# A two-layer f32 decoder trunk: the output projections in another order of products, loads and row sums

## The chip, the cores and the metric

The kernel runs on 1 core of one Trainium2 chip, in one launch. The metric is the device time in microseconds, lower is better. TensorE (PE) multiplies matrices into PSUM, VectorE (DVE) and ScalarE (ACT) work on tiles in SBUF and PSUM, GpSimd (POOL) issues transfers here and copies a little, and SyncE (SP) only issues transfers. Every engine takes its own instructions strictly in order and waits for the others through semaphores.

## The reference

The input is `x` of 512 tokens by 2048 channels in f32. Two layers follow, each of which adds a mixer's output to `x`:

```
x <- x + W_out( mixer(rms_norm(x)) * silu(gate) )
layer 0: gated differential attention, 8 heads of 256 value channels;
         o = rms_norm(o, subln_w) * (1 - lambda_init), per head
layer 1: RWKV-7 time mixing, 32 heads of 64 channels, group norm on y
```

What matters here is the end of each layer: `y` (512 x 2048) times `W_out` (2048 x 2048), plus the residual.

## The kernel before

**f32 products.** A product of f32 matrices is three matmuls of a faster format. Each operand is split into a high part (an ACT cast, `wh` for weights at L109, `hH` for rows at L475) and a low part (a DVE subtraction, `wl` at L110, `hL` at L476). `mm3` (L116) issues high x high, high x low, low x high; all of PE's matmul rows of a product bear its line, L118. Weights come from HBM in blocks of 256 by 512 (512 KB, tile `wraw`, three buffers in turn; `load_w`, issued at L76).

**The rows.** `y` comes turned, channel by token, in 16 row blocks of 128 channels by 512 tokens. All but the last come from HBM (`yd`, `yd2`), where the earlier heads left them, and `Feed` splits them ahead of use. The last two row blocks stay on the core. In layer 0 they are those of head 7, whose attention (`attention`, L386) is stepped through between the matmuls of the output projection by a `Chain`: for each of four token tiles scores, softmax, the product `o`, then `weigh` (L429: ACT squares `o`, DVE takes the root in 11 small operations through `rsqrt`, L58, and scales to `G` at L441), then `turn_y` (L443: PE transposes `G` into `yt` at L446, ACT copies it to the rows' tile `Tt` at L450). After all four tiles `split_row` (L471) splits the two row blocks whole, `hH` at L475. In layer 1 the last rows come from the last pair of heads: the last steps of the solver and the scan (which read the tiles `TT` and write `Y`), the group norm (`yc` scaled at L1757), transposes of `yc` at L1769, the gate, `split_row`.

**The output stage.** `outputs_of` (L916) makes the 2048 output columns in two halves, `one` (columns 0 to 1023) and `two`, each a `Blocks` (L804). A half is a two by two grid of places, tokens by columns: 11, 12, 21, 22 (256 tokens by 512 columns each). Of the 16 row blocks 12 go through a scheme with 7 products in place of 8 (three steps of two row blocks for each product, 36 matmuls) and 4 go plainly (`plain`, row blocks 6, 7 and 14, 15; 14 and 15 are the last rows). The 7 products are "11" and "12" (named for the block of rows that they use), "S1", "S2", "S4", "S3" (with sums of rows) and "22". `Forms` (L760) loads the rows for the sums (`load`, L770, on POOL's queue) and makes S1 to S4 (`make`, L773: DVE adds at L780, ACT and DVE splits at L793 and L794). The matching sums of weights grow in place in three tiles `Ts`: a transfer that adds to what lies there (`add_w`, L799, issued at L801), which only POOL's queue does here.

The order of the code is the order of the work on PE:

```
two.first12 / one.first12 alternately, one.first11, last rows (finish), S1 made,
one.rest: plain 6 c1, plain 14 c1, S1, plain 6 c2, plain 14 c2, S2, S4, S3, 22
two.first11, two.rest: the same again
```

(c1 and c2 are the half's two column blocks.) Between S4 and S3 stands nothing, and S3's first weights are the tile that S4 has just used, with one more block added by `add_w`.

**Residual.** The first product to reach a place writes it by `copy` (L836): an ACT copy from PSUM to SBUF, then a transfer on POOL's queue that adds `x` (layer 1: the stored `xd`) to it (L842). The others add by `take` (L845) on DVE, at L848.

Of the kernel before, what the change touches and what calls it, by code (L numbers as in the profile page):

```python
# [23 lines left out]
P = 128  # L24
# [33 lines left out]
def rsqrt(g, out, v, n, tag):  # L58
# [7 lines left out]
    for i in range(3):  # L66
        nc.vector.tensor_mul(t[:], y, y)
        nc.vector.scalar_tensor_tensor(t[:], t[:], -0.5, v, ALU.mult, ALU.mult)
        o = out if i == 2 else y
        nc.vector.scalar_tensor_tensor(o, t[:], 1.5, y, ALU.add, ALU.mult)  # L70

# [314 lines left out]
def attention(g, h, qkT, qkL, sq, vg, gap, rows=None, yT=None):  # L386
# [42 lines left out]
    def weigh(t):  # L429
# [9 lines left out]
        rsqrt(g, ro[:], so[:], 1, "r1")  # L439
# [13 lines left out]

    for i in range(NT + 3):
# [12 lines left out]
    if yT is not None:  # L467
        rows += [split_row(g, yT[:, c, :]) for c in range(2)]
# [14 lines left out]
class Feed:  # L483
# [17 lines left out]
    def __call__(self, n, m):  # L501
        self.split(n + 1, m)
        self.load(n + self.ring)

# [255 lines left out]
class Forms:  # L760


    def __init__(self, g, src, raws, homes):
        self.g, self.src, self.raws, self.homes = g, src, raws, homes
        self.at = {nm: [None] * len(homes) for nm in ("S1", "S2", "S3", "S4")}

    def load(self, i):
        for r, kb in zip(self.raws[i], (0, 1)):
# [4 lines left out]
    def make(self, nm):  # L773

        nc = self.g.nc
        for i, homes in enumerate(self.homes):
# [3 lines left out]
            nc.vector.tensor_tensor(out=o, in0=x, in1=y, op=op)  # L780
# [23 lines left out]
class Blocks:  # L804
# [26 lines left out]
    def plain(self, k0, c, *outs):  # L831
        wt = split_w(self.g, None, KG, 512, 0, self.load(k0, c))
        for out, t0, first, end in outs:
            self.products(out, self.block(k0, t0), wt, first, end)

    def copy(self, nm, ps, sign=1.0):  # L836
        nc, (t, c) = self.g.nc, PLACES[nm]
        with self.g.tc.high_priority(offset=SCAN):
            for i in range(2):
                nc.scalar.activation(self.acc(nm)[i], ps[i][:], AF.Copy, scale=sign)  # L840
                r0 = (2 * t + i) * P
                nc.gpsimd.dma_start(out=self.acc(nm)[i], accum_op=ALU.add,  # L842
                                    in_=self.x[r0 : r0 + P, self.c1 + c * 512 : self.c2 + c * 512])
# [6 lines left out]
    def first11(self, i):  # L850
        if not i:
            self.X = self.banks(0)
        load_w(self.g, self.Ts[i], self.w[self.c1 // 512], FIRST[0] + i * KG, slice(0, KG))
        self.prod(self.X, i, "11", self.Ts[i], i == 0, i == NS // KG - 1)
        add_w(self.g, self.Ts[i], self.w, FIRST[0] + i * KG, self.c2)
        if i == NS // KG - 1:
            self.take("11", self.X)

    def first12(self, i, bank):
        if not i:  # L860
            self.y = self.banks(bank)
        if i < NS // KG:
            self.prod(self.y, i, "12", self.load(FIRST[1] + i * KG, self.c1), i == 0)
        else:
            self.plain(PLAIN[0], self.c1, (self.y, 0, False, True))
            self.copy("11", self.y)

    def rest(self, begin=None, then=lambda nm: None):
# [5 lines left out]
        y, z = self.banks(1), self.banks(2)  # L874
# [4 lines left out]
        self.copy("21", z)  # L879
        then("S2")  # L880
        y, z = self.banks(1), self.banks(2)
# [3 lines left out]
        self.copy("22", y)  # L885
# [7 lines left out]
        self.copy("12", X, -1.0)  # L893
# [7 lines left out]
        self.done("12")  # L901
        for i in range(N):
# [4 lines left out]
        z = self.banks(2)  # L907
# [8 lines left out]
def outputs_of(g, one, two, feed, finish, begin=None):  # L916
# [6 lines left out]
    for i in range(N + 1):  # L923
        for x, (b, bank) in enumerate(((two, 0), (one, 1))):
            pace(s)
            b.first12(i, bank)
            s += KG
        if i == 1:
            one.sums.load(0)
    for i in range(N):  # L930
        pace(s)
        pace(s + 1)
        one.first11(i)
        s += KG
        if i:
            one.sums.load(i)
    finish(g.m)
    one.sums.make("S1")
    one.rest(then=one.sums.make)
    for i in range(N):  # L940
        two.first11(i)
# [3 lines left out]
def loader(g, w, homes):  # L945

    homes = list(homes)

    def load(k0, c):
        homes.append(homes.pop(0))  # L950
        pool, tag, bufs = homes[-1]
        raw = pool.tile([P, KG, 512], F32, name="wraw", tag=tag, bufs=bufs)
# [13 lines left out]
def layer0(g, aps):  # L966
# [3 lines left out]
    with ExitStack() as cx:  # L970
# [77 lines left out]
        with tc.issue_after(g.made[9][1]):  # L1048
            nc.vector.tensor_scalar(g.subw[:], g.subw[:], 1.0 - LAMBDA_INIT, None, ALU.mult)
# [4 lines left out]
    with ExitStack() as cx:  # L1054
# [22 lines left out]
        feed, rows = g.feed, g.feed.rows  # L1077
        ch = Chain(g, attention(g, NH - 1, *before, 20, rows, Tt[:, 4:6]), 8)
# [14 lines left out]
        def store_x(cb, t):  # L1093
            xr = xs[cb][:, t, :]
            junk = g.ps.tile([P, 512], F32, name="junkx", tag="pb")
# [12 lines left out]
        sums = Forms(g, g.yd, ((sx[0], sx[1]), (sx[2], Tt[:, 6:8]), (Tt[:, 0:2], Tt[:, 2:4])), homes)  # L1108
# [10 lines left out]
        def banks(i):  # L1119
            if i < 2:  # L1120
                return [g.pp.tile([P, 512], F32, name="pp", tag="pp") for _ in range(2)]
            return [g.ps.tile([P, 512], F32, name="z", tag="pa", bufs=2) for _ in range(2)]

        load = loader(g, aps["da_w_out"], ((g.wraw, "wraw", 3),))
# [42 lines left out]
        def begin(m):  # L1167
# [4 lines left out]
            for cb in range(1, 4):  # L1172
                for t in range(2):
# [4 lines left out]
                        [flat(g.C), flat(g.S), T2], banks, done_of(c)) for c in (0, 2)]  # L1178
# [795 lines left out]
```

## Time and profile before

| what | value |
|---|---|
| median of 3 runs | 2125.43 us (2124.93 to 2126.13) |
| profiled execution | 2125.24 us |
| its span, first to last instruction | 2123.1 us |
| mean granted clock of TensorE | 0.985 of full |
| busy: PE, DVE, ACT, POOL | 97%, 80%, 62%, 22% |
| layer 0's output stage | about 728 to 931 us |
| layer 1's output stage | about 1905 to 2118 us |

A row of a timeline gives start, duration, engine, line, operation, the tile written and those read, their shapes, and in brackets the time in which the engine was idle before it and whose instruction ended that. Matmuls overlap, so the pace is read from their starts. The granted clock is the share of full speed that PE was given in a stretch. A row of the windows view gives a stretch, its length, the busy time and count of PE, PE's weight loads, DVE, ACT and POOL, the clock, the mean busy share of the 16 DMA engines, and GB/s.

### The profile page before, as it was taken

Reading aid. Unit: us, or ns where it says so; the run is one execution under the profiler, and the core shown is the slowest. Engines: PE = TensorE matmul, PEld = TensorE weight load, DVE = VectorE, ACT = ScalarE, POOL = GpSimd, SP = SyncE. Lnnn points to the kernel's source line nnn. Section 1 sums busy time; section 2 is a strip of 40 time slices with the busy share of each in tenths; the row PEclk is TensorE's granted clock in tenths of the full one; section 3 lists DMA queues with packets and bytes.
Section 4 is the critical chain, followed back from the end, with each engine's and each line's share of the span. In section 5 each row is a group of like instructions: output and inputs, shape, how many; then the busy total and the mean of one; then the engine's idle time right before and its main releaser. Section 6 shows DMA issues by size and latency. Waiting matters only on the chain. (4 is left out here: it accounts for less than half of the span.)

```text
span 2123.1 us, 35355 instructions
## 1 busy us (share of the span) xinstructions
PE 2054.2 (97%) x11852; PEld 1686.2 (79%) x11852; DVE 1698.9 (80%) x4423; ACT 1317.8 (62%) x3119; POOL 471.3 (22%) x789
## 2 busy tenths in 40 slices
PE   9999999999999969999999999999999999997898
PEld 8878888888887857878778888888888888876676
DVE  5979788797888984576888888888888888887554
ACT  5667676676767754555666666666666666656343
POOL 0020220201203012201232322223222332333211
PEclk9999999999999989999999999999999999999899
DMA  6487887977879667952222222222222222246796
GB/s 197 118 168 181 160 176 176 172 180 158 185 175 221 197 147 155 215 134 91 77 73 78 78 78 75 80 81 78 83 77 83 74 83 77 91 143 164 161 215 141
DMA packets 104005, 281.23 MB, mean 132 GB/s; under 512 B 12848, under 2 KB 29376, under 8 KB 103824
## 3 DMA queue, kind: packets, MB, share of 16 engines
q0 software_dynamic: 32208, 99.21, 25.9%
q1 hardware_dynamic: 57184, 163.77, 24.4%
q10 hardware_dynamic: 14432, 16.01, 2.2%
q8 instruction: 93, 1.52, 0.3%
q14 instruction: 88, 0.72, 0.1%
HBM read 262.94 MB, written 15.99 MB: 131 GB/s over the span
## 5 line engine op out<-in xcount | busy, mean ns | idle before, releaser
L118 PE MATMUL pp<-hH,wh 128*128 128x512 f32 x1024 | 416.7, 407 | 0.0
L118 PE MATMUL pp<-hL,wh 128*128 128x512 f32 x1024 | 411.9, 402 | 0.0
L118 PE MATMUL pp<-hH,wl 128*128 128x512 f32 x1024 | 411.6, 402 | 0.0
L109 ACT CAST wh<-wraw 128x512 fp32r<-128x512 f32 (+1 forms) x408 | 250.3, 618 | 205.5 <-PE pp L118 110.3
L110 DVE TENSOR_TENSOR wl<-wraw,wh 128x512 fp32r<-128x512 f32 (+1 forms) x408 | 289.0, 711 | 101.7 <-ACT wh L109 96.2
L118 PE MATMUL pp<-wh,hH 128*128 128x512 f32 x696 | 278.0, 400 | 12.2 <-ACT wh L109 8.5
L118 PE MATMUL pp<-wl,hH 128*128 128x512 f32 x696 | 275.4, 396 | 0.8 <-DVE wl L616 0.6
L118 PE MATMUL pp<-wh,hL 128*128 128x512 f32 x696 | 273.8, 394 | 0.0
L118 PEld LDWEIGHTS pp<-hH,wh 128*128 128x128 f32 x1024 | 192.8, 188 | 38.0 <-issue 2.1
L118 PEld LDWEIGHTS pp<-hH,wl 128*128 128x128 f32 x1024 | 193.1, 189 | 33.3
L118 PEld LDWEIGHTS pp<-hL,wh 128*128 128x128 f32 x1024 | 193.1, 189 | 31.3
L118 PE MATMUL pp<-wh,S 128*128 128x512 f32 x672 | 214.7, 395 | 0.0
L615 ACT CAST wh<-T 128x512 fp32r<-128x512 f32 x224 | 137.3, 621 | 93.6 <-PE pp L118 71.7
L1686 POOL COPY SA<-VS 64x64 f32<-64x64 f32 x224 | 77.0, 344 | 510.8 <-DVE VS L1704 456.1
L616 DVE TENSOR_TENSOR wl<-T,wh 128x512 fp32r<-128x512 f32 x224 | 150.9, 687 | 24.9 <-ACT wh L615 24.2
L118 PEld LDWEIGHTS pp<-wh,hH 128*128 128x128 f32 x696 | 131.5, 189 | 40.5 <-ACT wh L109 8.9
L588 POOL DMA_DIRECT2D T<-in_da_w_in_dram x84 | 72.2, 859 | 387.5 <-DMA wraw<-in_da_w_in_dram 193.8
L118 PEld LDWEIGHTS pp<-wl,hH 128*128 128x128 f32 x696 | 131.7, 189 | 26.8 <-DVE wl L110 1.1
L118 PEld LDWEIGHTS pp<-wh,hL 128*128 128x128 f32 x696 | 131.8, 190 | 26.6
L1551 DVE SCALAR_TENSOR_TENSOR tmpl<-LT,n,Tm 128x60 f32<-128x60 f32 (+24 forms) x496 | 135.8, 274 | 13.4
L118 PEld LDWEIGHTS pp<-wh,S 128*128 128x128 f32 x672 | 124.7, 188 | 24.7 <-ACT wh L615 0.4
L118 PE MATMUL pp<-wl,S 128*128 128x512 f32 x336 | 132.1, 393 | 0.2 <-DVE wl L616 0.2
(380 smaller groups left out, 4335.2 us busy)
## 6 DMA issues: line engine op xcount, KB each, us to landing
wraw<-in_rw_w_in_dram SPq DMA_DIRECT2D x128, 512.0 KB, 3.7
T<-in_da_w_in_dram POOLq DMA_DIRECT2D x84, 512.0 KB, 6.5
wraw<-in_da_w_in_dram SPq DMA_DIRECT2D x64, 512.0 KB, 4.1
T<-in_da_w_in_dram SPq DMA_DIRECT2D x28, 512.0 KB, 4.4
wraw<-in_da_w_out_dram SPq DMA_DIRECT2D x22, 512.0 KB, 5.6
wraw<-in_rw_w_out_dram SPq DMA_DIRECT2D x22, 512.0 KB, 4.5
wraw<-in_da_w_in_dram POOLq DMA_DIRECT2D x21, 512.0 KB, 6.7
TT<-in_rw_w_out_dram POOLq DMA_DIRECT2D x12, 512.0 KB, 5.8
```

The costliest lines, as they stand in the source:

```text
L109: nc.scalar.copy(hi[:], raw[:, k : k + n])
L110: g.split = nc.vector.tensor_sub(lo[:], raw[:, k : k + n], hi[:].bitcast(F32)).ins
L118: m = nc.tensor.matmul(out, a, b, start=s, stop=e, skip_group_check=skip)
L588: self.g.nc.gpsimd.dma_start(out=raw, in_=src, accum_op=ALU.add)
L615: g.nc.scalar.copy(hi[:], raw[:, k])
L616: g.nc.vector.tensor_sub(lo[:], raw[:, k], hi[:].bitcast(F32))
L1551: st = nc.vector.scalar_tensor_tensor(tt, LT[:, i : i + 1, i + 1 :].to_broadcast([P, s, n]), n2[:, i : i + 1], Tm[:, 0:s, i : i + 1].to_br ...
L1686: nc.gpsimd.tensor_copy(p.SA[r_, c - 1, :], VS[r_, c, h, :])
```

## The change

1. The order. Both halves' "12" and "11" products now come before the last rows; the 36 matmuls of `two.first11` are new in that place. S1 is made after them.
2. The last rows of layer 0 are split in two halves of 256 tokens (`split_tail`), and the second half's steps are taken between the two parts of `plain` 14 (`between`). In layer 1 the last rows' steps begin after the second of `two.first11`'s three steps.
3. The rows for the sums are loaded on SP's queue, after `one.first11`.
4. The residual is loaded plainly into the place (`want`, on SP's queue), and all products add to it by `take`. `copy` is gone.
5. `plain` 14 c2 moves from before S2 to between S4 and S3; its weights have a buffer of their own.
6. `two`'s first weight blocks are loaded twice: once into `wraw` for its "11", later into freed tiles to grow its sums from (`begin_sums`).
7. In layer 1 the tiles `Ts` go in the order TT[0], a third tile, TT[1]; before, TT[0], TT[1], the third. PSUM banks are assigned by name.
8. In layer 0's `weigh` the root has 8 operations (`rsqrt_column`), and its constant factor is in `subw`.

The number of matmuls stays. The core of the diff:

```diff
+def rsqrt_column(g, out, v):
...
+    for i, c in enumerate((3.0, 12.0, 768.0)):
+        nc.vector.scalar_tensor_tensor(t[:], y, y, v[:], ALU.mult, ALU.mult)
+        o = out[:] if i == 2 else y
+        nc.vector.scalar_tensor_tensor(o, t[:], -c, y, ALU.add, ALU.mult)
...
+    def split_tail(t0):
...
+            nc.scalar.copy(hh[:, s], yT[:, c, s])
+            g.rowsplit = nc.vector.tensor_sub(hl[:, s], yT[:, c, s], hh[:, s].bitcast(F32)).ins
+
     for i in range(NT + 3):
         if i > 2:
             turn_y(i - 3)
+        if i == 4:
+            split_tail(0)
...
-    if yT is not None:
-        rows += [split_row(g, yT[:, c, :]) for c in range(2)]
+    split_tail(2)
...
-            self.g.nc.gpsimd.dma_start(
+            self.g.nc.sync.dma_start(
                 out=r, in_=self.src[k0 * P : (k0 + KG) * P, :].rearrange("(k p) t -> p k t", p=P))
...
-    def copy(self, nm, ps, sign=1.0):
...
+    def want(self, *names):
+        for nm in names:
+            t, c = PLACES[nm]
+            for i, a in enumerate(self.acc(nm)):
                 r0 = (2 * t + i) * P
...
+                self.g.nc.sync.dma_start(out=a, in_=self.x[r0 : r0 + P, self.c1 + c * 512 : self.c2 + c * 512])
...
+    def begin_sums(self):
+        for i, T in enumerate(self.Ts):
+            load_w(self.g, T, self.w[self.c1 // 512], FIRST[0] + i * KG, slice(0, KG))
+            add_w(self.g, T, self.w, FIRST[0] + i * KG, self.c2)
...
         self.plain(PLAIN[0], c1, (z, 256, True, False))
-        self.plain(PLAIN[1], c1, (y, 0, True, True), (z, 256, False, True))
+        finish(False)
+        self.want("21", "22")
+        y = self.banks("y")
+        self.plain(PLAIN[1], c1, (y, 0, True, True), (z, 256, False, True), between=lambda: finish(True))
...
-        for n, k0 in enumerate(PLAIN):
-            self.plain(k0, c2, (z, 256, n == 0, n == 1), (y, 0, False, False))
-        self.take("22", z)
+        z = self.banks("z")
+        self.plain(PLAIN[0], c2, (z, 256, True, False), (y, 0, False, False))
+        self.want("12")
...
-            self.prod(y, i, "S4", b22[i], end=i == last)
+            self.prod(y, i, "S4", b22[i])
             add_w(g, b22[i], w, FIRST[0] + i * KG, c2)
+        self.plain(PLAIN[1], c2, (z, 256, False, True), (y, 0, False, True))
...
+        if next:
+            next.Ts = [self.sums.raws[i][j] for i, j in ((0, 0), (0, 1), (1, 0))]
+            next.begin_sums()
...
     for i in range(N):
-        two.first11(i)
+        one.sums.load(i)
+    for i in range(N):
+        two.first11(i, False)
+        if i == 1:
+            finish(None)
+    two.take("11", two.X)
+    one.sums.make("S1", g.m.ins)
+    one.rest(None, one.sums.make, finish, two)
     two.rest(begin)
...
-        Ts = [flat(x) for x in g.TT] + [g.low.tile([P, KG, 512], F32, name="T2", tag="SX", bufs=3)[:]]
+        Ts = [flat(g.TT[0]), g.low.tile([P, KG, 512], F32, name="T2", tag="SX", bufs=3)[:], flat(g.TT[1])]
```

Three places show how the instructions move. The first is PE in layer 0 at the last token tile of head 7, before the change: `o` is the tile's last product, `yt` the transposes of its result `G`, and `pp` and `hH` the plain product with the last rows.

```order
L118 MATMUL o_8797<-V_8226,at_8757 128x256
L118 MATMUL o_8797<-VL_8227,at_8757 128x256
L118 MATMUL o_8797<-V_8226,al_8758 128x256
L446 MATMUL yt_8829<-ident_82,G_8228 128x128 x2
L118 MATMUL pp_8855<-wh_8883,hH_8834 128x512
L118 MATMUL pp_8855<-wl_8884,hH_8834 128x512
```

The same place after the change, where `z_8833` is a plain product with earlier rows and `z_8862` the product that follows the transposes:

```order
L133 MATMUL o_8699<-V_8142,al_8663 128x256
L133 MATMUL pp_8742<-wh_8802,hH_8603 128x512
L133 MATMUL pp_8742<-wl_8803,hH_8603 128x512
L133 MATMUL pp_8742<-wh_8802,hL_8604 128x512
L133 MATMUL z_8833<-wh_8837,hH_7762 128x512
L133 MATMUL z_8833<-wl_8838,hH_7762 128x512
L133 MATMUL z_8833<-wh_8837,hL_7763 128x512
L133 MATMUL z_8834<-wh_8837,hH_7762 128x512
L133 MATMUL z_8834<-wl_8838,hH_7762 128x512
L133 MATMUL z_8834<-wh_8837,hL_7763 128x512
L133 MATMUL z_8833<-wh_8841,hH_7766 128x512
L133 MATMUL z_8833<-wl_8842,hH_7766 128x512
```

Before, the transposes stood directly behind the last `o`; now 15 matmuls stand between (three more `z` follow the rows shown, then `yt_8777`).

The second place is DVE around the same root, after the change. `rs_t`, `rs_i` and `ro` are the root's small operations, `G` its result, `wl` weight splits, `Tt` at L819 and `fS1` at L833 the sum S1, `xq` at L887 an add to the output.

```order
L85 SCALAR_TENSOR_TENSOR ro_8644<-rs_t_8646,rs_i_8645 128x1
L819 TENSOR_TENSOR Tt_8163<-frow_8175,Tt_8163 128x2x256
L455 SCALAR_TENSOR_TENSOR ro_8644<-ro_8644,r_8476,hrstd0_596 128x1
L125 TENSOR_TENSOR wl_8842<-wraw_8835,wh_8841 128x512
L456 SCALAR_TENSOR_TENSOR G_8144<-o_8631,ro_8644,G_8144 128x256
L833 TENSOR_TENSOR fS1_8826<-Tt_8163,fS1_8826 128x512
L887 TENSOR_TENSOR xq_8167<-xq_8167,pp_8741 128x512
L125 TENSOR_TENSOR wl_8866<-wraw_8863,wh_8865 128x512
L819 TENSOR_TENSOR Tt_8163<-Tt_8163 128x2x256
L452 TENSOR_SCALAR so_8712<-so_8712 128x1
L887 TENSOR_TENSOR xq_8168<-xq_8168,pp_8742 128x512
L79 TENSOR_SCALAR rs_i_8716<-so_8712 128x1
```

Sums, weight splits and an output add stand among the root's steps of the last two token tiles; S1 now starts between the two roots.

The third place is SP's queue in layer 0 after the change. `wraw` are weight blocks, `Tt<-yd` rows for the sums, `xq` the residual.

```order
L91 DMA wraw_8743<-in_da_w_out_dram 128x1024
L808 DMA Tt_8163<-yd_78 128x2x512
L91 DMA wraw_8765<-in_da_w_out_dram 128x1024
L91 DMA wraw_8796<-in_da_w_out_dram 128x1024
L808 DMA Tt_8163<-yd_78 128x2x512
L882 DMA xq_8165<-in_x_dram 128x512 x4
L882 DMA xq_8166<-in_x_dram 128x512 x4
L91 DMA wraw_8835<-in_da_w_out_dram 128x1024
L808 DMA Tt_8163<-yd_78 128x2x512
L91 DMA wraw_8863<-in_da_w_out_dram 128x1024
```

Rows for the sums and eight residual loads stand among the weight blocks on SP; before, both of these went through POOL's queue, the residual as transfers that add.

More of the change, by code (lines that the diff above doesn't have):

```diff
@@ L923, in outputs_of @@
     for i in range(N + 1):
-        for x, (b, bank) in enumerate(((two, 0), (one, 1))):
+        for b in (one, two):
             pace(s)
-            b.first12(i, bank)
+            if i == N - 1 and b is two:
+                b.want("11")
+            b.first12(i)
             s += KG
-        if i == 1:
-            one.sums.load(0)
+    two.take("11", two.y)
     for i in range(N):
@@ L1076, in layer0, with finish @@
         g.spare = lambda k: Tt[:, (0, 1, 2, 3, 6, 7)[k % 6]]
[L1077 to L1078 removed]
+        feed = g.feed
+        tail = []
+        ch = Chain(g, attention(g, NH - 1, *before, 18, tail, Tt[:, 4:6]), 8)
+        def finish(whole):
+            while whole is False and not tail:
+                ch.step(g)
+            if whole:
+                ch.finish(g)
+        rows = RowList(feed.rows, tail)
         g.ssx = g.const.tile([P, NT, 4], F32, name="ssx")
@@ L1117, in done_of, with banks, of @@
             return done
[L1119 to L1124, printed above, removed]
+        def banks(places):
+            def of(nm):
+                where = places[nm]
+                if where == "pp":
+                    return [g.pp.tile([P, 512], F32, name="pp", tag="pp") for _ in range(2)]
+                return [g.ps.tile([P, 512], F32, name="z", tag=t, bufs=where.count(t)) for t in where]
+            return of
+        load = loader(g, aps["da_w_out"], lambda: Tt[:, 4:6])
         rs = g.work.tile([P, NT], F32, name="rs1", tag="al", bufs=1)
```

150 lines of the change are left out of this document (87 added, 63 removed).

## The prediction

> **What bounds the kernel now.** I read the page first, then the timeline of TensorE (PE) over both output stages, then the windows around its gaps, then the timelines of VectorE (DVE), ScalarE (ACT) and GpSimd (POOL), and the DMA view, for what ended each gap. The page: engine, busy time, share; and the granted clock in 40 slices.
>
> ```profile
> PE 2054.2 (97%) x11852; PEld 1686.2 (79%) x11852; DVE 1698.9 (80%) x4423; ACT 1317.8 (62%) x3119; POOL 471.3 (22%) x789
> PEclk9999999999999989999999999999999999999899
> ```
>
> PE is the bound, idle for 2123.1 - 2054.2 = 69 us in all. The two digits of the clock that fall to 8 stand where the two output stages begin, so the question is how much of the idle time lies there. The timeline of PE (start, duration, operation; in brackets the idle time before it and who ended it), layer 0 first, from the row at 1957 on layer 1:
>
> ```profile
> 773.53 0.39 PE L118 MATMUL z<-wh,hL 128*128 128x512 f32 x1
> 787.70 0.66 PE L446 MATMUL yt<-ident,G 128*128 128x128 f32 x2 [13.78 <-DVE G L441]
> 790.50 0.41 PE L118 MATMUL o<-V,al 128*128 128x256 f32 x1
> 794.81 0.66 PE L446 MATMUL yt<-ident,G 128*128 128x128 f32 x2 [3.89 <-DVE G L441]
> 796.69 0.79 PE L118 MATMUL pp<-wh,hH 128*128 128x512 f32 x1 [1.22 <-ACT hH L475]
> ...
> 845.13 0.80 PE L118 MATMUL pp<-wh,fS 128*128 128x512 f32 x1 [2.69 <-ACT wh L109]
> ...
> 918.57 0.49 PE L118 MATMUL pp<-wh,fS 128*128 128x512 f32 x1 [2.89 <-ACT wh L109]
> ...
> 1957.63 0.80 PE L118 MATMUL pp<-wh,hH 128*128 128x512 f32 x1 [8.46 <-ACT wh L109]
> ...
> 1978.52 1.12 PE L1769 MATMUL pt<-ident,yc 128*128 128x128 f32 x4 [6.13 <-DVE yc L1757]
> 1982.33 0.79 PE L118 MATMUL pt<-wh,hH 128*128 128x512 f32 x1 [2.69 <-ACT hH L475]
> ...
> 2028.98 0.56 PE L118 MATMUL pp<-wh,fS 128*128 128x512 f32 x1 [2.30 <-ACT wh L109]
> ...
> 2102.91 0.49 PE L118 MATMUL pp<-wh,fS 128*128 128x512 f32 x1 [3.23 <-ACT wh L109]
> ```
>
> Layer 0 waits 13.78 + 3.89 + 1.22 + 2.69 + 2.89 = 24.5 us here, layer 1 8.46 + 6.13 + 2.69 + 2.30 + 3.23 = 22.8: 47.3 of the 69. In each layer the first ones come from the last rows (of the last head, of the last turn), the last two are the first S3 product of each column half.
>
> A gap also costs clock. Two rows with 36 matmuls from the one to the other give the full pace, (869.10 - 860.94) / 36 = 0.2267 us each; the windows give the pace behind the gaps (stretch, its length, PE busy and count, PEld, DVE, ACT, POOL, granted clock, DMA share, GB/s):
>
> ```profile
> 860.94 0.39 PE L118 MATMUL pp<-wh,hH 128*128 128x512 f32 x1
> 869.10 0.39 PE L118 MATMUL z<-wh,hH 128*128 128x512 f32 x1
> ```
>
> ```profile
> 728.00:797.00 69.00, 48.26 (x234) 38.70 (x233) 57.32 (x166) 42.23 (x97) 9.14 (x11) 0.85 0.62 160
> 797.00:931.00 134.00, 128.00 (x535) 103.21 (x535) 68.73 (x118) 62.41 (x118) 27.70 (x34) 0.96 0.85 186
> 787.70:802.20 14.50, 9.39 (x32) 7.62 (x33) 8.30 (x23) 5.07 (x13) 0.00 (x0) 0.56 0.00 0
> 845.10:850.20 5.10, 5.00 (x14) 3.41 (x15) 3.36 (x6) 3.46 (x8) 0.00 (x0) 0.69 0.88 211
> 918.50:924.50 6.00, 5.70 (x17) 4.28 (x18) 5.40 (x16) 4.15 (x10) 0.00 (x0) 0.72 0.73 169
> 1957.60:1962.00 4.40, 4.37 (x64) 3.27 (x65) 2.69 (x5) 2.16 (x4) 2.18 (x3) 0.61 0.23 25
> 1978.50:1990.00 11.50, 8.79 (x25) 6.81 (x26) 7.04 (x11) 4.04 (x7) 1.74 (x2) 0.57 0.27 61
> 2028.90:2034.00 5.10, 4.86 (x14) 3.64 (x15) 3.72 (x7) 2.30 (x6) 0.00 (x0) 0.67 0.67 156
> 2102.90:2108.50 5.60, 5.36 (x15) 4.02 (x16) 4.33 (x7) 2.64 (x5) 0.00 (x0) 0.70 0.31 105
> 1905.00:1990.00 85.00, 65.31 (x435) 50.49 (x435) 61.92 (x139) 45.90 (x101) 27.04 (x39) 0.86 0.62 165
> 1990.00:2118.00 128.00, 122.08 (x517) 98.75 (x516) 62.95 (x96) 50.16 (x84) 25.97 (x30) 0.97 0.84 182
> ```
>
> Busy time less count times 0.2267 is what the low clock cost: 2.1 at 787, 1.8 at 845, 1.85 at 918, 3.1 at 1978, 1.7 at 2029, 2.0 at 2103; at 1957, where the matmuls are small, (1 - 0.61) x 4.37 = 1.7. Sum 14.3. So the gaps that the change touches are worth 47.3 + 14.3 = 61.6 us, 30.3 in layer 0 and 31.3 in layer 1.
>
> What ends them (DVE, then the chain that ended last with its landing weight load, then a row of Y products):
>
> ```profile
> 781.70 0.69 DVE L780 TENSOR_TENSOR Tt<-Tt 128x512 f32<-128x512 f32 x1 [5.67 <-DMA Tt<-yd]
> 791.61 0.15 DVE L437 TENSOR_SCALAR so<-so 128x1 f32<-128x1 f32 x1 [1.05 <-ACT o L436]
> 791.80 0.15 DVE L63 TENSOR_SCALAR rs_i<-so 128x1 int32<-128x1 int32 x1
> 794.18 0.48 DVE L441 SCALAR_TENSOR_TENSOR G<-o,ro,G 128x256 f32<-128x256 f32 x1
> 1973.75 0.69 DVE L780 TENSOR_TENSOR frow<-frow 128x512 f32<-128x512 f32 x1 [3.74 <-DMA frow<-yd]
> ```
>
> ```profile
> 1948.71 8.22 DMA TT<-in_rw_w_out_dram
> ```
>
> ```profile
> 1959.08 2.03 PE L1724 MATMUL Y<-VS,G 128*64 128x64 f32 x32
> ```
>
> **The change part by part.** *Sums' rows later.* At 781.70 DVE, which works in order, has stood 5.67 us for the rows of the sums, with root operations of the last token tile but one queued behind it; the same in layer 1 at 1973.75. Now S1 is made after the second half's "11" product, so nothing of the last rows stands behind that load. The 13.78 and the 6.13 lose their cause.
>
> *The extra product.* 36 matmuls, 8.16 us at full pace, move ahead of the last rows with 12 plain ones split between the halves. They are no new work (PE's count stays), only cover. From the last product "o" (790.50 + 0.41) to the transposes at 794.81 the chain takes 3.9 us; 15 matmuls, 3.4 us, stand there now. The root is three operations shorter at 791.80 - 791.61 = 0.19 each: 0.6. That would close the gap, but in the new DVE order six large operations of about 0.69 (weight splits, sums, a residual add) stand among the root's: up to 4.1 back. Bounds 0 to 4, plus up to 2 of clock; I take 5, nearest to the 3.89 that the same chain cost before.
>
> *SP's queue.* Eight residual loads (256 KB each, 2.1 MB) and sums' rows stand ahead of the weight block for the plain product that covers the last rows. The DMA view of 797 to 931 (packets, MB, share of the 16 engines' time):
>
> ```profile
> q0 software_dynamic: 4608, 13.63, 59.2%
> q1 hardware_dynamic: 2160, 7.47, 17.8%
> ```
>
> By it a plain load on SP's queue takes 0.178 x 134 / 7.47 = 3.2 us per MB of all engines, POOL's queue 0.592 x 134 / 13.63 = 5.8. So 2.1 MB hold that block back by 6.7 us at most; it has been wanted only after some 8 us of matmuls. Bounds 0 to 5; I take 3. For the first residual adds (their PSUM banks come free only then) I take 2, for the start of the second half 1. **Layer 0 keeps 5 + 3 + 2 + 1 = 11 (4 to 16).**
>
> *S3 gaps.* S3 needs a weight sum whose accumulating DMA POOL can issue only after S4's split; it had S4's 36 matmuls to hide behind, now 24 more, 5.4 us. The waits were 2.30 to 3.23, so they go, with their clock. The cost is on the other side: S1 to S2 shrinks from 84 to 60 matmuls, 13.6 us, the distance S3 has now too; I expect no wait there.
>
> *Layer 1's TT[1].* The buffer is read by the last solver step, and its load (8.22) was wanted at once. It is now third in the row: 14 matmuls (3.2) and the Y products (2.0 by the row at 1959.08) later, 5.2 us of cover. 8.46 - 5.2 = 3.3 is left; with a landing like the median of the page below, 5.6 and not 8.22, it is 0.7. I take 2, and 1 of clock. The other last rows: 1 for the transposes, 1 for the split row, 1 for residual adds. **Layer 1 keeps 6 (3 to 11).**
>
> *Residual.* 16 ACT copies and 16 accumulating loads per layer become plain loads and DVE adds. DVE is busy 68.7 of 134 us in the stage, so the adds of 0.69 hide; POOL is freed of 16 issues. Transfer time falls by 4.2 MB x (5.8 - 3.2) = 11 us per layer, if the price goes with the queue; the three weight loads that are made again add 1.6 x 3.2 = 5. The page's DMA issues (count, KB, median us to landing), and DVE's waits for residuals in 770 to 931 (total, times, longest):
>
> ```profile
> wraw<-in_da_w_out_dram SPq DMA_DIRECT2D x22, 512.0 KB, 5.6
> TT<-in_rw_w_out_dram SPq DMA_DIRECT2D x4, 512.0 KB, 5.6
> xq<-in_x_dram POOLq DMA_DIRECT2D x16, 256.0 KB, 6.6
> DVE xq L848 <- DMA xq<-in_x_dram: 6.5, 4, 3.1
> ```
>
> [...] The two queue rows differ by 1.8 times, but q0's transfers are partly accumulations, so the rows do not say whether queue or kind sets the price.
>
> *Clock.* The row at 845.10 shows 0.69 behind a gap of 2.69 us, and the other S3 gaps 0.67 to 0.72 behind 2.30 to 3.23. [...]
>
> **Sum.** 61.6 - 11 - 6 = 44.6 us. The profiled execution took 2125.24 (span 2123.1 and 2.1 around it), 0.2 below the median of 2125.43. 2125.24 - 44.6 = 2080.6; I say 2080.
>
> **The rivals.**
>
> *Forecast, 0.76:* 2064 (all 61.6 gone) to 2094.
>
> *A. The transfers bind, 0.10.* For: the share is 0.85 and 0.84 in the two late windows, and the 20 idle us around the last rows, in which loads ran ahead, go. Layer 0's stage moves 69 x 0.62 + 134 x 0.85 = 157 us of transfers, layer 1's 85 x 0.62 + 128 x 0.84 = 160. If the plain loads keep POOL's price, each gets 1.6 MB x 5.8 = 9 more; at 0.85, the highest share shown, that takes 195 and 199 us. The stages would be 203 - 30 + 11 = 184 and 213 - 31 + 6 = 188. Loss 11 + 11 = 22, the time **2103**. Against: plain loads looked cheaper.
>
> *B. The slow pace behind the short gaps belongs to the place, 0.02.* [...]
>
> *C. Slower: a convoy on SP, 0.05.* Each of the 16 places (four in each half, two halves, two layers) now adds its residual only after a plain load that stands in SP's one queue among weight blocks, and these wait in turn for buffers that PE frees. If PE's banks hang on such an add, PE waits for SP, which waits for PE's last block. Before, DVE waited at most 3.1 us for a residual. At 4 us a place it costs 64, and the time is 2080 + 64 = **2144**; it decides from 45 / 16 = 2.8 us a place. Against: the accumulators are free early, so most loads can be issued long before.
>
> *D. The change doesn't cover the last rows, 0.07.* The chain from "o" to the transposes and TT[1] wait as long as before because DVE and SP have more queued ahead of them. Then only the S3 gaps go, 2.69 + 2.89 + 2.30 + 3.23 + 7.35 = 18.5: **2107**.
>
> **How the numbers follow.** The likeliest is 2080. From 2064 to 2104 lie the forecast, B, and about half of A: a little over 8 in 10, leaving out the rest of A, C and D. About 0.2%, 4.3 us, is what a measurement of this kernel can tell from no change. Only C lies above 2125 + 4.3, at 0.05; 0.02 of D, in which more is put in the way of the last rows than before, ends within 0.2%, the rest below: faster 0.93, same 0.02, slower 0.05.
>
> **What would show it.** Right: no wait over 5 us on PE in either stage; none before the S3 products; a granted clock above 0.9 where it was 0.85 and 0.86; PE's idle total near 35 us. Each step is wrong if: the transposes still wait over 6 us for G (D); the weight split of TT[1] still ends 5 us or more of idle; the S1 or S2 products get waits of 2 us or more; the rows behind the residual loads are ended by DMA at several places (A or C); the DMA share rises above 0.9 with waits on wraw spread through the stage (A). The prediction is wrong as a whole if the gaps go and the time does not.

## The result and the profile after

The changed kernel takes 2086.83 us (median of 4 runs, 2086.57 to 2089.86); before, in the same runs, 2125.18 (2122.44 to 2126.13). The ratio is 0.9825, with a 95% interval of 0.9808 to 0.9842: 38.4 us faster. The profiled execution took 2086.84, its span 2085.1, so the traces are 38.0 apart. 2080 was forecast, with a range of 2064 to 2104.

The page of the changed kernel, engines and clock:

```profile
PE 2048.9 (98%) x11852; PEld 1682.4 (81%) x11852; DVE 1712.8 (82%) x4361; ACT 1301.7 (62%) x3089; POOL 432.3 (21%) x745
PEclk9999999999999999999999999999999999999999
```

The count on PE is the same, its idle time went from 69 to 2085.1 - 2048.9 = 36.2 us, and the two 8s of the clock are gone. Another 5.3 us came off PE's busy time, with the same count of matmuls; the mean granted clock is 0.993, 0.985 before. The timeline of PE has these waits in the two output stages of the changed kernel, layer 0 to the row at 841, then layer 1:

```profile
771.19 0.80 PE L133 MATMUL pp<-wh,hH 128*128 128x512 f32 x1 [2.86 <-DVE xq L887]
773.40 0.66 PE L461 MATMUL yt<-ident,G 128*128 128x128 f32 x2 [1.42 <-DVE G L456]
793.74 0.41 PE L461 MATMUL yt<-ident,G 128*128 128x128 f32 x2 [2.44 <-DVE G L456]
841.85 0.49 PE L133 MATMUL pp<-wh,fS 128*128 128x512 f32 x1 [2.27 <-ACT wh L124]
...
1937.54 0.77 PE L133 MATMUL pp<-wh,hH 128*128 128x512 f32 x2 [2.01 <-ACT wh L124]
1951.43 0.66 PE L1840 MATMUL pt<-ident,yc 128*128 128x128 f32 x4 [0.92 <-DVE yc L1828]
2000.41 0.79 PE L133 MATMUL pp<-wh,fS 128*128 128x512 f32 x1 [4.39 <-ACT wh L124]
```

13.78 became 1.42, 3.89 became 2.44, 8.46 became 2.01 and 6.13 became 0.92. Of the four S3 waits (rows with `fS` and ACT's weight split) those of the second half are gone, but those of the first half are still there: 2.69 became 2.27, and in layer 1 2.30 became 4.39. A wait of 2.86 us at 771 is new. The windows right behind the waits of the changed kernel (stretch, length, PE busy and count, PEld, DVE, ACT, POOL, granted clock, DMA share, GB/s):

```profile
771.00:777.00 6.00, 4.39 (x17) 3.89 (x18) 5.49 (x15) 1.91 (x7) 0.86 (x1) 0.50 0.87 218
793.70:798.00 4.30, 4.26 (x13) 3.42 (x14) 2.04 (x5) 2.44 (x6) 0.29 (x1) 0.61 0.89 173
797.00:893.00 96.00, 93.50 (x400) 75.98 (x399) 62.71 (x100) 46.47 (x86) 17.02 (x22) 0.98 0.85 195
841.80:847.00 5.20, 4.91 (x14) 3.71 (x15) 3.86 (x7) 3.73 (x10) 0.00 (x0) 0.67 0.65 189
1937.50:1942.00 4.50, 4.46 (x12) 3.27 (x13) 3.68 (x8) 2.69 (x5) 0.85 (x1) 0.62 0.85 252
1960.00:2080.00 120.00, 115.61 (x490) 93.33 (x489) 75.05 (x119) 46.94 (x78) 17.24 (x20) 0.97 0.80 186
2000.40:2006.00 5.60, 5.59 (x13) 4.14 (x13) 3.16 (x6) 1.62 (x3) 0.42 (x1) 0.50 1.05 225
```

What the low clock still costs, as busy time x (1 - clock): 2.2 at 771, 1.7 at 793, 1.6 at 841, 1.7 at 1937, 2.8 at 2000.

POOL's queue in layer 0 suggests why S3 still waits; the first experiment tests it. `wraw` rows are the three adds whose sums S3 multiplies by, `frow` rows the first adds of the second half's sums, which the change begins here; in brackets POOL's idle time before:

```profile
815.58 0.87 POOL L840 DMA_DIRECT2D frow<-in_da_w_out_dram  x1 [2.70 <-DMA frow<-in_da_w_out_dram]
...
819.71 0.84 POOL L840 DMA_DIRECT2D frow<-in_da_w_out_dram  x1 [2.00 <-DMA frow<-in_da_w_out_dram]
824.85 0.86 POOL L840 DMA_DIRECT2D T<-in_da_w_out_dram  x1 [4.29 <-DVE xq L887]
827.32 0.86 POOL L840 DMA_DIRECT2D wraw<-in_da_w_out_dram  x1 [1.61 <-DVE wl L125]
830.18 0.87 POOL L840 DMA_DIRECT2D frow<-in_da_w_out_dram  x1 [2.00 <-issue]
832.61 0.84 POOL L840 DMA_DIRECT2D wraw<-in_da_w_out_dram  x1 [1.56 <-issue]
835.60 0.86 POOL L840 DMA_DIRECT2D wraw<-in_da_w_out_dram  x1 [2.14 <-issue]
```

One `frow` add stands between the adds that S3 needs, others before them, and two of them make POOL wait for their own loads (2.70 and 2.00 us). The second of the `wraw` adds, issued at 832.61, is the one that PE waits for: ACT starts on its tile at

```profile
841.18 1.14 ACT L124 CAST wh<-wraw 128x512 fp32r<-128x512 f32 x2 [4.65 <-DMA wraw<-in_da_w_out_dram]
```

The new wait at 771 begins on DVE, which stands for the residual's load at the first two adds of the first half (the root's steps and the scaling to G are behind it in DVE's order):

```profile
766.57 0.69 DVE L887 TENSOR_TENSOR xq<-xq,pp 128x512 f32<-128x512 f32 x1 [1.43 <-DMA xq<-in_x_dram]
...
770.45 0.69 DVE L887 TENSOR_TENSOR xq<-xq,pp 128x512 f32<-128x512 f32 x1 [3.05 <-DMA xq<-in_x_dram]
```

### The profile page after: what moved, and what is told of

Read it like the earlier page. It is cut to its first block, busy times and chain, and to the rows that moved or that the text cites. A ratio compares the mean times of both kernels' runs of the same rounds, so it can differ in the third digit from the quotient of the medians.

```text
span 2085.1 us, 35228 instructions
## 1 busy us (share of the span) xinstructions
PE 2048.9 (98%) x11852; PEld 1682.4 (81%) x11852; DVE 1712.8 (82%) x4361; ACT 1301.7 (62%) x3089; POOL 432.3 (21%) x745
## 3 DMA queue, kind: packets, MB, share of 16 engines
q8 instruction: 93, 1.52, 0.3%
## 5 line engine op out<-in xcount | busy, mean ns | idle before, releaser
L124 ACT CAST wh<-wraw 128x512 fp32r<-128x512 f32 (+1 forms) x416 | 255.6, 618 | 217.4 <-PE pp L133 121.2
L125 DVE TENSOR_TENSOR wl<-wraw,wh 128x512 fp32r<-128x512 f32 (+1 forms) x416 | 294.7, 711 | 89.6 <-ACT wh L124 84.1
L133 PE MATMUL pp<-wh,hH 128*128 128x512 f32 x684 | 272.4, 399 | 5.8 <-DVE xq L887 2.9
L133 PE MATMUL pp<-wl,hH 128*128 128x512 f32 x684 | 270.3, 395 | 0.8 <-DVE wl L653 0.6
```

Of the source, the lines that this page charges most:

```text
L124: nc.scalar.copy(hi[:], raw[:, k : k + n])
L125: g.split = nc.vector.tensor_sub(lo[:], raw[:, k : k + n], hi[:].bitcast(F32)).ins
L133: m = nc.tensor.matmul(out, a, b, start=s, stop=e, skip_group_check=skip)
```

## The experiments

The main theory is the prediction's: each wait of PE has a cause of its own, and the time moves with the waits and the clock behind them. What it didn't have was why S3 still waits; the rivals are that the 16 DMA engines are full there, that 24 matmuls of cover are too few, or that the order on POOL's queue decides. Before the change took 2124.2, 2125.3 and 2125.5 us in the three sets of runs below, against which the ratios are; each time is a median of 4 runs (of 10 where said). The intervals are some 3 to 5 us to either side, so two of these kernels that are less than about 5 us apart are not told from each other by their times.

**The begun sums added last.** The adds of `begin_sums` are put behind S3's on POOL's queue; all else and all bytes stay.

```diff
-            add_w(self.g, T, self.w, FIRST[0] + i * KG, self.c2)
+            with self.g.tc.issue_after(after):
+                add_w(self.g, T, self.w, FIRST[0] + i * KG, self.c2)
...
-            next.begin_sums()
+            next.begin_sums(added.ins)
```

> The changed kernel, with only the order on POOL's queue altered: the three weight sums that are begun for the second half (begin_sums) are added behind the three adds that S3 waits for, not among them. Theory (POOL's queue sets S3): the waits of 2.27 us (layer 0) and 4.39 us (layer 1) before the second S3 step of the first half fall below 1, and so does the low clock behind them (5.2 us at 0.67, 5.6 us at 0.50, worth 1.7 and 2.8); 2087 falls by 8 to 11, to 2076 to 2079. Rival (the 16 DMA engines are full there): the same bytes must pass in the same stretch, the waits keep more than half of their length or come back before the second half's first S1 product; the time stays within 3 of 2087.

Measured: 2078.2 us (2077.55 to 2079.7), ratio 0.9783 (0.9767 to 0.98), 8.6 less than the changed kernel. The S3 waits and their clock were 11.1; small waits elsewhere are longer (1.92 for `yc` in place of 0.92). POOL's timeline of this kernel, same place:

```profile
825.23 0.85 POOL L840 DMA_DIRECT2D wraw<-in_da_w_out_dram  x1 [1.85 <-DMA frow<-in_da_w_out_dram]
828.64 0.86 POOL L840 DMA_DIRECT2D wraw<-in_da_w_out_dram  x1 [2.56 <-DVE wl L125]
830.92 0.86 POOL L840 DMA_DIRECT2D wraw<-in_da_w_out_dram  x1 [1.43 <-DVE wl L125]
833.40 0.87 POOL L840 DMA_DIRECT2D frow<-in_da_w_out_dram  x1 [1.61 <-issue]
```

and its windows over the same lengths as above:

```profile
797.00:893.00 96.00, 96.00 (x415) 78.57 (x415) 66.01 (x104) 49.09 (x91) 17.46 (x22) 0.98 0.88 203
1950.00:2070.00 120.00, 120.00 (x525) 98.25 (x526) 83.92 (x132) 50.42 (x83) 18.06 (x21) 1.00 0.81 197
```

PE has no idle time left in either stretch, at a mean DMA share of 0.88 and 0.81, about as high as where it waited. Around S3's adds the share was higher, in the changed kernel and in this one, in that order:

```profile
826.00:842.00 16.00, 13.73 (x60) 10.79 (x59) 4.74 (x8) 3.63 (x7) 3.44 (x4) 1.00 1.06 233
...
824.00:842.00 18.00, 18.00 (x81) 14.83 (x80) 11.20 (x17) 7.84 (x16) 5.14 (x6) 1.00 1.06 239
```

A mean share of 1.06 is full by this measure. So the rival's premise holds and its conclusion does not: the engines are full there in both kernels, and PE waits in one alone. The order decides which bytes come first.

**The second plain product of c2 back before S2** (part 5 of the change undone):

```diff
-        self.plain(PLAIN[0], c2, (z, 256, True, False), (y, 0, False, False))
+        for n, k0 in enumerate(PLAIN):
+            self.plain(k0, c2, (z, 256, n == 0, n == 1), (y, 0, False, False))
...
-        self.plain(PLAIN[1], c2, (z, 256, False, True), (y, 0, False, True))
```

> The changed kernel with one part undone: the second plain product of column block c2 stands before S2 again and no longer between S4 and S3. Theory (24 matmuls, 5.4 us, are the cover of S3's adds): the first half's S3 waits grow by 5.4 in each layer, the second half's come back at about the 2.9 and 3.2 us that they had before; 10.8 + 6.1 of idle time and some 4 of clock, 2087 rises by 17 to 22, to 2104 to 2109. Rival (the second half's waits went because the residual's adding transfers no longer stand ahead of S3's adds on POOL's queue): the second half gets no wait over 1 us, only the first half's grow; the rise is 10 to 14, to 2097 to 2101.

Measured: 2094.15 (2092.46 to 2096.25), ratio 0.9856 (0.9842 to 0.9871), 7.3 more than the changed kernel, less than either expected. PE's waits at S3 in this kernel are two, both in the first halves:

```profile
838.99 0.80 PE L133 MATMUL pp<-wh,fS 128*128 128x512 f32 x1 [4.57 <-ACT wh L124]
...
2007.52 0.79 PE L133 MATMUL pp<-wh,fS 128*128 128x512 f32 x1 [7.15 <-ACT wh L124]
```

They grew by 2.3 and 2.8, not 5.4, and the second halves have none. So the 24 matmuls are not needed for the second halves' waits to go. As to the place the rival is right.

**Both edits together**, begun sums last and the plain product back (both diffs above):

> The edits of the first and third run together: the second half's three begun sums are added last, and the second plain product of c2 stands before S2 again, so that nothing stands between S4 and S3. Theory A (what stands ahead on POOL's queue sets S3, the 24 matmuls do nothing once the queue is right): no S3 wait over 1 us in either half, the time within 3 of the 2078 of the first run. Theory B (the prediction's: 24 matmuls, 5.4 us, are the cover): S3 waits of 2 to 5 us come back, the time is 2083 to 2096.

Measured: 2079.75 (2079.24 to 2082.28), ratio 0.9792 (0.9772 to 0.9811); 1.5 above the first run. No S3 wait in either half, with nothing between S4 and S3. That is theory A: part 5 of the change is worth nothing once POOL's queue is in order, and only half covers a queue that isn't.

**And the residual of the places 12 by adding transfers again** (on top of the kernel just told):

```diff
-        self.want("12")
...
-        self.take("12", X, ALU.subtract)
+        self.copy("12", X, -1.0)
```

> As the run before in this list, and besides the residual of the places 12 is added as before the change: ACT copies PSUM, and a transfer on POOL's queue adds x, just ahead of the adds that S3 waits for. Theory A (the residual's adding transfers on POOL's queue made the S3 waits before the change): all four S3 waits come back at 2 to 4 us with some 1.7 of clock each, the time is 14 to 22 above that run. Rival (POOL's queue keeps up, and the waits went for another reason): under 4 above it.

Measured: 2098.66 (2095.73 to 2100.14), ratio 0.9877 (0.9856 to 0.9897); 18.9 more than without. PE's timeline of this kernel has all four S3 waits again, and POOL's shows two adds of the residual between those that S3 needs:

```profile
844.80 0.49 PE L133 MATMUL pp<-wh,fS 128*128 128x512 f32 x1 [2.35 <-ACT wh L124]
908.96 0.49 PE L133 MATMUL pp<-wh,fS 128*128 128x512 f32 x1 [1.52 <-ACT wh L124]
...
2012.24 0.49 PE L133 MATMUL pp<-wh,fS 128*128 128x512 f32 x1 [2.28 <-ACT wh L124]
2076.68 0.51 PE L133 MATMUL pt<-wh,fS 128*128 128x512 f32 x1 [1.49 <-ACT wh L124]
```

```profile
830.55 0.84 POOL L840 DMA_DIRECT2D wraw<-in_da_w_out_dram  x1 [1.80 <-DVE wl L125]
831.85 0.86 POOL L890 DMA_DIRECT2D xq<-in_x_dram  x1 [0.45 <-ACT xq L888]
833.59 0.86 POOL L890 DMA_DIRECT2D xq<-in_x_dram  x1 [0.89 <-ACT wh L124]
836.62 0.87 POOL L840 DMA_DIRECT2D wraw<-in_da_w_out_dram  x1 [2.17 <-issue]
```

The waits are a little shorter than expected (1.5 to 2.35), the time is inside what was expected. They make 7.6 us. The 5.1 to 5.8 us behind each ran at a clock of 0.67 to 0.71, by busy time x (1 - clock) 6.5 more, 14.1 in all; the other 4.8 were not placed. The second of S3's adds is issued 6.1 us behind the first, 3.1 in the kernel without these residual adds (827.62 and 830.77), and ACT starts on its tile 7.5 us later (844.13), 5.8 there (836.55). So the place in the queue is the larger part; that the residual's adds are also more for the engines to do (a mean share of 0.82 over 797 to 893 in this kernel) is not separated from it.

**The 36 matmuls held behind the last rows' transposes.** The edit also steps layer 0's chain to its end at once (`finish(True)`), which the expectation does not count:

```diff
+    finish(None)
+    finish(True)
+    with one.g.tc.issue_after(one.g.turned):
-    for i in range(N):
-        two.first11(i, False)
-        if i == 1:
-            finish(None)
+        for i in range(N):
+            two.first11(i, False)
```

> The changed kernel with the second half's product 11 (36 matmuls) held on PE until the last rows' transposes have been issued, in both layers; all else stays, S1's sums after it too. Theory (these 36 matmuls, 8.2 us, are the cover of the last rows): in layer 0 the last transposes wait 3 to 5 in place of 2.44 and the ones before wait more, in layer 1 the transposes of yc wait 3 to 9 in place of 0.92; with the clock 2087 rises by 9 to 18, to 2096 to 2105. Rival (the sums that stood in DVE's way were all of it, and their move alone brought the gain): the rise is under 4.

Measured: 2102.62 (2100.97 to 2103.95), ratio 0.9897 (0.9873 to 0.992); 15.8 more than the changed kernel. PE's waits for the last three token tiles of layer 0 and for `yc` in layer 1, in this kernel:

```profile
775.88 0.66 PE L461 MATMUL yt<-ident,G 128*128 128x128 f32 x2 [5.76 <-DVE G L456]
786.99 0.66 PE L461 MATMUL yt<-ident,G 128*128 128x128 f32 x2 [5.77 <-DVE G L456]
...
789.79 0.41 PE L133 MATMUL o<-V,al 128*128 128x256 f32 x1
793.69 0.66 PE L461 MATMUL yt<-ident,G 128*128 128x128 f32 x2 [3.48 <-DVE G L456]
...
1960.13 1.12 PE L1841 MATMUL pt<-ident,yc 128*128 128x128 f32 x4 [8.92 <-DVE yc L1829]
```

The waits and the time are the theory's, but the cover that was taken away is more than the 36 matmuls: in layer 0 the transposes at 793.69 stand directly behind the last `o` at 789.79, so the 15 matmuls that the change had put there are gone too. And the wait at S3 is gone in layer 0 and 2.65 in layer 1 here, so 15.8 is what is left of a larger loss. The cover as a whole is the largest part of the gain that was undone in the changed kernel; the share of the extra product in it is not shown.

**TT[1] second again:**

```diff
-        Ts = [flat(g.TT[0]), g.low.tile([P, KG, 512], F32, name="T2", tag="SX", bufs=3)[:], flat(g.TT[1])]
+        Ts = [flat(x) for x in g.TT] + [g.low.tile([P, KG, 512], F32, name="T2", tag="SX", bufs=3)[:]]
```

> The changed kernel with the weight tiles of layer 1 in the old order, TT[1] second. Theory (the 14 matmuls and the Y products are the cover of its load): the wait of 2.01 us at its first use goes back to 7 to 9, the time rises by 5 to 8, to 2092 to 2095. Rival (the third tile's load is then as late, or TT[1] comes earlier now that SP's queue is another): the rise is under 2.5.

Measured: 2092.09 (2090.44 to 2096.22), ratio 0.985 (0.9828 to 0.9872); 5.3 more. It waits at two places, 4.13 where it waited 2.01, and 2.58 for a weight split where it did not wait:

```profile
1933.90 0.80 PE L133 MATMUL pp<-wh,hH 128*128 128x512 f32 x1 [4.13 <-ACT wh L124]
1950.19 0.50 PE L133 MATMUL pt<-wl,hH 128*128 128x512 f32 x1 [2.58 <-DVE wl L125]
```

The size is as expected, but at the border of what the times can tell; that the wait at the tile itself went back to 7 to 9 is not what happened. Nor is that wait steady: in the other runs that keep the new order it was 1.98 to 3.62, so how much of the 5.3 is the order of the tiles is not shown.

**The rows for the sums on SP, alone, in the kernel before:**

```diff
-            self.g.nc.gpsimd.dma_start(
+            self.g.nc.sync.dma_start(
                 out=r, in_=self.src[k0 * P : (k0 + KG) * P, :].rearrange("(k p) t -> p k t", p=P))
```

> The kernel before the change with one part of it alone: the rows for the sums are loaded on SP's queue. In layer 0 the order on PE and DVE stays as it is. Theory (on POOL's queue the rows come late, and DVE, in order, stands 5.67 us for them with the root behind): DVE's stand at the sums falls below 2, the wait of 13.78 us on PE by 4 or more, 2125 falls by 5 to 15. Rival (the rows' buffer comes free late, whichever queue loads it): the stand stays within 2 of 5.67, the time within 4 of 2125.

Measured: 2120.95 (10 runs, 2113.11 to 2123.44), ratio 0.9976 (0.9963 to 0.9989). The rows of DVE and PE in this kernel that answer to 5.67 and 13.78:

```profile
778.53 0.69 DVE L780 TENSOR_TENSOR Tt<-Tt 128x512 f32<-128x512 f32 x1 [1.51 <-DMA Tt<-yd]
```

```profile
784.53 0.66 PE L446 MATMUL yt<-ident,G 128*128 128x128 f32 x2 [9.62 <-DVE G L441]
```

The stand fell by 4.16 and PE's wait by 4.16: that part of 13.78 was the rows' lateness. The time fell by 4.6, just short of the 5 expected. That the other 9.62 are the sums and the chain themselves, with nothing to cover them, is argued and not shown. In layer 1 the edit brought little: DVE stood 4.83 us for these rows at 1965.98, 3.74 before, and PE's 6.13 became 3.77 for a weight split and 2.08 for `yc`, 5.85 in all.

**The opposite edit in the changed kernel**, these loads on POOL again:

```diff
-            self.g.nc.sync.dma_start(
+            self.g.nc.gpsimd.dma_start(
                 out=r, in_=self.src[k0 * P : (k0 + KG) * P, :].rearrange("(k p) t -> p k t", p=P))
```

> The changed kernel with the opposite edit: the rows for the sums on POOL's queue again. Theory: these loads stand among POOL's adds and DVE's sums wait for them again; where the S1 sums stand among the last root's operations the transposes wait 2 to 6 us more, the time rises by 3 to 10, to 2090 to 2097. Rival (which queue issues makes no difference, as all use the same engines, and S1 is wanted late now): within 3 of 2087.

Measured: 2096.83 (2090.36 to 2099.76), ratio 0.9865 (0.9844 to 0.9886); 10 more than the changed kernel by the median, with an unusually wide spread. The profiled run is the fastest of the four, 2090.36. In layer 0 no sum waits there; DVE has a longer wait for the residual (5.00 in place of 3.05), which PE felt as 2.87 in place of 2.86. In layer 1 DVE stands twice for the rows of the sums, 5.9 us in place of one stand of 1.44:

```profile
1897.07 0.69 DVE L819 TENSOR_TENSOR frow<-frow 128x512 f32<-128x512 f32 x1 [3.70 <-DMA frow<-yd]
...
1950.53 0.69 DVE L819 TENSOR_TENSOR frow<-frow 128x512 f32<-128x512 f32 x1 [2.17 <-DMA frow<-yd]
```

After them PE waits 1.62 and 1.65 at 1899 and 1901, and 1.64 for `yc` in place of 0.92. So the theory's mechanism is there, in the other layer than the last root of layer 0. This trace is only 3.5 us longer than the changed kernel's; what the slower three lost isn't in a trace and stays open.

**The long root** (11 operations) in the changed kernel:

```diff
-        rsqrt_column(g, ro, so)
+        rsqrt(g, ro[:], so[:], 1, "r1")
```

> The changed kernel with the root of 11 operations in the attention again. Theory (the root is short against what stands among it): 3 x 0.19 = 0.6 us on each chain that PE waits for, three of them in the last two heads; the time rises by 0 to 2, to 2087 to 2089. Rival (the saving is worth its 32 x 3 x 0.19 = 18 us of DVE on the path): the rise is 6 or more. Second rival (the new order on DVE that the shorter root brought made the wait of 2.46 us with a clock of 0.72 behind it in the head before the last): the time falls by 1 to 3.

Measured: 2090.12 (2088.83 to 2091.8), ratio 0.9837 (0.9823 to 0.9852); 3.3 more. Between the theory's 0 to 2 and the rival's 6. PE waits 3.42 and 3.83 for the last two tiles there, 3.95 in the head before (2.46 in the changed kernel), and no longer at 771: the order on DVE changed with it, so the 3.3, which the times barely tell from nothing, are not the root's 0.6 per tile alone. The second rival falls, as the time did not.

**One place's residual by an adding transfer**, only the first of layer 0 (ACT copies PSUM, POOL adds x):

```diff
-        if not i:
+        if not i and begin:
+            one.copy("11", one.y)
+        elif not i:
             one.want("11")
```

> The changed kernel, with the residual of one place (11 of the first half, layer 0 only) added as before the change: ACT copies PSUM to the tile and a transfer adds x to it, so that PSUM's banks come free without waiting for the residual's load. Theory (DVE stands for 1.43 and 3.05 us on that load, with the head's scaling behind it): PE's waits of 2.86 and 1.42 us at 771 to 773 go, and the clock of 0.50 behind them; the time falls by 4 to 7, to 2080 to 2083. Rival (the last head's chain is late anyway): the wait moves to the transposes at 773 as DVE's weight splits and the scaling stay in the way; the fall is under 2.

Measured: 2084.43 (2083.91 to 2086.86), ratio 0.9812 (0.9798 to 0.9827); 2.4 less, between the two. The waits of 2.86 and 1.42 went, but waits of 1.87 for a weight split and 1.84 for G came. In layer 1, which the edit does not touch, the wait for `TT` was 3.62 in place of 2.01 and S3's 3.01 in place of 4.39: single waits move that much without an edit in their layer. Then **this and the begun sums last, together:**

> The edits of the first and second run together: the begun sums added last on POOL's queue, and the residual of one place of layer 0 added by a transfer. Theory (separate waits, so the gains add): 2078 less the 2.4 of the second run, 2074 to 2077. Rival (the second run's 2.4 came from S3 waits that were shorter in it, 1.14 and 3.01, which are gone here): 2077 to 2081.

Measured: **2072.22** (2070.79 to 2073.18), ratio 0.9754 (0.9737 to 0.977), the fastest kernel here: 53.3 below before in the same set of runs (2125.51), 14.6 below the changed kernel. That is 6.0 below the first run, more than the 2.4 that this edit gave alone; of the 6.0 between the traces 1.9 are the wait for `yc` in layer 1, which this edit does not touch and which is gone here; why the rest is more than 2.4 isn't shown.

## Why the prediction was right, and where it was not

The forecast's sum was 61.6 - 11 - 6. The 61.6 stands up: what the changed kernel still waits and loses to clock in these places, 61.6 - 38.0 = 23.6, is close to the 16.3 of idle time in the seven rows and the 10.0 of clock behind five of them, 26.3. What was off is how much would be left, 26 in place of 17, and it was off in one step above all. That the forecast came within 7 us is in part luck: the S3 waits and the first residual adds left 15.5 more than was priced, and the other terms, SP's queue above all, left 6.2 less.

- *S3 gaps, the step that failed.* The prediction said that 24 more matmuls, 5.4 us, cover waits of 2.30 to 3.23, "so they go". In the first halves they did not: 2.27 + 1.6 and 4.39 + 2.8 of clock are left, 11 us priced at nothing. And in the second halves they went for another reason. The plain product put back leaves them at nothing; the residual's adds put back as well bring all four. The cause was what stands ahead of S3's adds on POOL's queue. The change cleared the residual's adds from it and put `begin_sums`' there. The prediction had counted these three tiles as 5 us of transfers and not as places in POOL's queue, though it priced the places in SP's queue for the loads that moved there.
- *The extra product.* 5 was left for the transposes, 2.44 + 1.7 is. From the last `o` (787.58 + 0.28) to the transposes at 793.74 the chain takes 5.9 us, 3.9 before, so the large operations of DVE among the root's came at a price, as was said, and ate some 2 of the 3.4 us of cover. The cover in all, with the plain matmuls of layer 0, is worth 15.8 net.
- *SP's queue.* 3 and 1 were left for the plain product's block and the second half's start; neither waits.
- *First residual adds.* 2 was left, 2.86 + 1.42 + 2.2 is. DVE stands 1.43 and 3.05 us for the load. This is rival C's mechanism at one place of 16, not a convoy.
- *Layer 1's TT[1] and last rows.* 3 was left, 2.01 + 1.7 is; 1 for the transposes, 0.92 is; the 2 for the split row and the residual did not come.
- *The sums' rows.* Half right: the load's lateness was 4.2 of the 13.78, and of the 6.13 in layer 1 it is shown for next to nothing. Without the cover the transposes wait again, 5.77 and 8.92 us. And the first of these sums, in the head before the last, still holds up DVE: 4.29 us at 687.32 (2.80 before) and PE 2.46 at 688.56 (1.96 at 689.24), with a clock of 0.72 over 690 to 694 where it was 1.00.
- *Rival A* (transfers bind) falls for the stage: with the same bytes PE does not idle at all over 96 and 120 us, at shares of 0.88 and 0.81. Its 0.85 was also not the highest share in the prediction's own rows (0.88 at 845). Around S3's adds, over 16 and 18 us at 1.06, the engines are full; there the order decides who waits. *Rival B* (with the clock behind the four S3 gaps kept, 1.8 + 1.85 + 1.7 + 2.0 = 7.35 us: 2088) falls: in the first run the S3 waits of layer 1 are gone, and the clock over that stretch is 1.00. *Rival D* falls with the transposes at 1.42 and 2.44 and TT[1] at 2.01.

By the prediction's own tests: no wait over 5 us, idle 36.2 (about 35), a clock of 0.93 and 0.98 over the stretches that had 0.85 and 0.86, and S1 and S2 without waits were right; "none before the S3 products" was wrong.

## What to carry to other kernels

List for each queue what stands ahead of the transfer that someone waits for, before and after the change, and count a step that is moved in every queue it uses: bytes that fit into the stage as a whole (a share of 0.85 here) can still stand ahead of those that are waited for, where the engines are full for a while (1.06 over 16 us here). A wait that goes may go for another reason than the cover that was put there; undo the cover alone, look in the trace whether it was that alone, and see. Price a wait together with the clock behind it (2.8 us behind 4.39 here).

## What the runs showed of the hardware that was not expected

The length of a gap alone does not decide whether the clock falls. The wait for `TT` in layer 1 was 2.01 us in the changed kernel, and the 4.5 us from 1937.50 on ran at 0.62 (12 matmuls). With the begun sums added last it was 2.02 us, and the same length ran at 1.00 (19 matmuls):

```profile
1935.89 0.73 PE L133 MATMUL pp<-wh,hH 128*128 128x512 f32 x2 [2.02 <-ACT wh L124]
...
1935.90:1940.40 4.50, 4.50 (x19) 3.42 (x20) 4.22 (x10) 3.19 (x6) 0.85 (x1) 1.00 0.86 253
```

And behind the shortest S3 waits with the residual's adds back, 1.52 and 1.49 us, it ran at 0.67 and 0.68:

```profile
908.90:914.00 5.10, 4.81 (x13) 3.51 (x14) 4.54 (x12) 3.63 (x9) 0.00 (x0) 0.67 0.80 175
...
2076.60:2082.00 5.40, 5.10 (x14) 3.83 (x15) 4.36 (x7) 2.50 (x6) 0.00 (x0) 0.68 0.35 114
```

So a gap of 1.5 to 2 us costs some 1.6 us of clock or nothing, and what decides it is not shown here. The prediction put up to 2 us of clock on a wait; 2.2 at 771 and 2.8 at 2000 are more, and behind the 2.02 us it was nothing. The windows at 771 and 2000 ran at 0.50, and none shown here ran lower. The clock fell behind gaps of 1.49, 1.52 and 2.01 to 2.44 us as well as behind the longer ones.

Adding transfers in a row are slow to come: of the three `wraw` adds of the changed kernel the median from issue to landing was 8.5 us, 6.1 for the two plain `wraw` loads of SP in the same stretch (826 to 845), and POOL issued them 5.3 (with one `frow` add between) and 3.0 us apart, where one issue takes 0.86. The same loads on SP in place of POOL took 4.6 us off the kernel before, and on POOL in place of SP added 10 by the median to the changed one. The bytes are the same; part of it is seen as stands of DVE for these loads (4.16 us less in layer 0, 4.4 more in layer 1), and the rest is not traced.
